# Rotating a matrix: half of one of the last outputs leaves through GpSimd in strips of seven partitions

## The chip, the core and the metric

One core of a Trainium2 chip runs the kernel. The metric is the time of one execution on the device, in microseconds (us), as the median of several runs; a profile of one execution shows where the time goes. The core has a matrix engine (TensorE, "PE" in the profile, with its weight loads as "PEld"), a vector engine (VectorE, "DVE"), ScalarE ("ACT"), GpSimd ("POOL") and SyncE ("SP"), and 16 DMA engines that move data between the DRAM and the on-chip memory (SBUF, 128 partitions). PSUM is the memory into which TensorE writes.

## The reference

```python
def setup_inputs():
    return {"x": np.random.randn(8192, 8192).astype(np.float32), "k": 1}

def reference(x, k):
    return np.rot90(x, k)
```

The 8192 x 8192 matrix of 4-byte numbers (268.4 MB) is turned by a quarter counterclockwise: `out[i, j] = x[j, 8191 - i]`. Nothing is computed. All of it is read once and written once, and within the chip each block is mirrored and transposed.

## The kernel before

**Tiles.** The input is cut into 16 macro blocks of R = 1024 rows by W = 4096 columns (`macros`, numbered kk). A macro block is loaded as T = 8 row strips of 128 rows, 2 MB each (`load`, L157), and leaves as J = 8 outputs of 2 MB. A strip consists of J = 8 pieces of CH = 512 columns; piece j of all 8 strips makes output j, so an output needs the whole macro block.

**Stages.** SyncE issues the loads into five buffers (`bufs`; LAND = 2 for loads, OUTS = 3 for outputs, with the roles mixed at the beginning and end by `load_buf` and `out_buf`). VectorE copies each strip piece by piece in reversed column order into `ring` (L209), which has 63 slots of 512 columns. TensorE transposes 128 x 128 blocks of the ring into PSUM (L241), 32 to an output, in two halves `ps0` and `ps1`. ScalarE copies each half to an output buffer (L272) and, when both are there, issues the store (L277). Semaphores order all of it: `s_land` for loads, `s_rev` for the reversed copies, `s_half` for a half transposed, `s_ev` for a half copied out, `s_store` for stores that have landed.

**The last macro block.** Its outputs are cut the other way so that work can begin with the first four strips: `outs` ends with t = 0 to 3 and columns j = (0, 1), (2, 3), (4, 5), (6, 7), and then t = 4 to 7 with the same columns. Each of these eight covers 1024 rows by 512 columns of the result, again 2 MB; partition m of the output buffer holds eight result rows m, m + 128 and so on, of 2 KB each. In an output with `js[0] == 0` the transposes are sorted by strip (L250), otherwise by block. The eight outputs use five buffers in turn (`ends` in `out_buf`), so the sixth, seventh and eighth wait at L268 for the store that used their buffer. These eight are "the last outputs" below, the fifth of them being the first one with t = 4 to 7.

**DMA.** `whole_reads` (L32) rewrites each load's and store's source so that a partition's 16 KB are read as one run. `LINE` and `HEAD` place the buffers in SBUF: `HEAD` is the width of the tile with the identity matrix, and the buffers' addresses are multiples of `LINE` bytes.

**GpSimd** writes the identity matrix (L174, L176) at the start and has nothing to do after that. SyncE ends with waits for every buffer's stores (L192).

Of the kernel before, what the change touches and what calls it, by code (L numbers as in the profile page):

```python
# [6 lines left out]
P = 128  # L7
# [5 lines left out]
G = 4  # L13
J = W // (G * P)
# [3 lines left out]
CH = G * P  # L18
F = G * R
SLOTS = T * J - 1  # L20

END = T // 2

H = 2
LAND = 2
OUTS = 3

LINE = 1024
HEAD = 224


def whole_reads(nc):  # L32

    for fn in nc.m.functions:
        for block in fn.blocks:
            for n, ins in enumerate(block.instructions):
                if not isinstance(ins, mybir.InstDMACopy):
                    continue
                src = ins.ins[0]
                ap = [list(d) for d in src.ap]  # L40
                if len(ap) == 3 and ap[2][0] == 1 and ap[1][0] == ap[2][1]:
# [12 lines left out]


def kernel(tc: tile.TileContext, x: bass.AP, k: bass.AP, out: bass.AP):
    nc = tc.nc
# [3 lines left out]
    N, M = x.shape  # L61
    dt = x.dtype
    macros = [(r0, c0) for r0 in range(0, N, R) for c0 in range(0, M, W)]
# [8 lines left out]
    for t in range(0, T, END):  # L72
        for j in range(0, J, wide):
            outs.append((KK - 1, range(t, t + END), range(j, j + wide)))
    assert len(outs) == n_out


    order = [(kk, a, b) for kk in range(KK) for a in range(T) for b in range(J)]
# [5 lines left out]
    with tc.tile_critical():  # L84
        head = nc.alloc_sbuf_tensor("head", [P, HEAD], dt)
        ident, scratch = head[:, :P], head[:, P : P + 1]
        bufs = [nc.alloc_sbuf_tensor(f"buf{i}", [P, F], dt) for i in range(LAND + OUTS)]
        ring = nc.alloc_sbuf_tensor("ring", [P, SLOTS * CH], dt)
        for b in bufs:
            assert nc.lookup_mloc(b).addr % LINE == 0  # L90
        ps = [
# [8 lines left out]
        s_first = nc.alloc_semaphore("s_first")  # L100
        s_half = nc.alloc_semaphore("s_half")
        s_ev = nc.alloc_semaphore("s_ev")

        def load_buf(m):
            if m < T:
# [1 line left out]
            return LAND + 2 if m == T else (m - T - 1) % LAND  # L107

        def out_buf(n):
            e = n - (n_out - J)  # L110
            if e < 0:
                return LAND + (n + 1) % OUTS
            ends = [load_buf(n_load - 2)]
            ends += [LAND + (n_out - J + i + 1) % OUTS for i in range(OUTS)]
            ends += [load_buf(n_load - 1)]
            return ends[e % len(ends)]

# [52 lines left out]
        with nc.Block() as block:  # L170

            @block.gpsimd
            def _(e):
                e.memset(ident, 0.0).then_inc(s_id, 1)  # L174
                e.wait_ge(s_id, 1)
                e.affine_select(  # L176
                    out=ident,
                    in_=ident,
                    compare_op=mybir.AluOpType.not_equal,
                    fill=1.0,  # L180
                    base=0,
                    pattern=[[-1, P]],
                    channel_multiplier=1,
                ).then_inc(s_id, 1)

            @block.sync
            def _(e):
                for m in range(LAND + OUTS, n_load):
                    last = [i for i in range(m) if load_buf(i) == load_buf(m)]
                    e.wait_ge(s_rev, rev[last[-1], J - 1])  # L190
                    load(e, m)
                for b in range(LAND + OUTS):  # L192
                    n = sum(out_buf(i) == b for i in range(n_out))
                    if n:
                        e.wait_ge(s_store[b], 16 * n)

            @block.vector
            def _(e):
                for m in range(n_load):
                    kk, t = divmod(m, T)  # L200
                    b = load_buf(m)
                    a = bufs[b][:].rearrange("p (j c) -> p j c", c=CH)
                    e.wait_ge(s_land[b], 16 * (uses_before(m, load_buf) + 1))
                    for lo, hi, wait in pieces[m]:
                        if wait:
# [12 lines left out]

            @block.tensor
            def _(e):  # L220
                seen = {}

                def wait(sem, n):
                    if seen.get(sem, 0) < n:
                        seen[sem] = n
                        e.wait_ge(sem, n)

                e.wait_ge(s_id, 2)
                for n, (kk, ts, js) in enumerate(outs):
                    blocks = [(j, g) for j in reversed(js) for g in range(G)]  # L230
                    half = len(blocks) // H
                    rows = len(ts) * P

                    def transpose(t, b):
                        j, g = blocks[b]
                        if n:
                            wait(s_ev, H * (n - 1) + b // half + 1)
                        wait(s_rev, rev[kk * T + t, j])
                        at = slot(kk, t, j) * CH + g * P
                        f = b % half * rows + (t - ts[0]) * P  # L240
                        i = e.transpose(  # L241
                            ps[b // half][:, f : f + P], ring[:, at : at + P], ident
                        )
                        if t == ts[-1] and b % half == half - 1:
                            i.then_inc(s_half, 1)
                        elif t == ts[0] and b == len(blocks) - 1:
                            i.then_inc(s_first, 1)

                    order = [(t, b) for b in range(len(blocks)) for t in ts]
                    if js[0] == 0:  # L250
                        order.sort()
                    for t, b in order:
                        transpose(t, b)

            @block.scalar
            def _(e):
                e.wait_ge(s_id, 2)
                e.copy(scratch, ident[:, :1])  # L258
                for n, (kk, ts, js) in enumerate(outs):
                    r0, c0 = macros[kk]  # L260
                    rows = len(ts) * P
                    b = out_buf(n)
                    for h in range(H):
                        if h == 0:
                            stores = uses_before(n, out_buf)
                            loads = [i for i in range(n_load) if load_buf(i) == b]
                            if stores:
                                e.wait_ge(s_store[b], 16 * stores)  # L268
# [3 lines left out]
                        e.copy(  # L272
                            bufs[b][:, h * F // H : (h + 1) * F // H], ps[h][:]
                        ).then_inc(s_ev, 1)
                    top = M - c0 - (js[-1] + 1) * CH
                    e.wait_ge(s_ev, H * (n + 1))
                    e.dma_start(  # L277
                        out=out[
                            top : top + len(js) * CH, r0 + ts[0] * P : r0 + ts[0] * P + rows
                        ].rearrange("(g m) f -> m g f", m=P),  # L280
                        in_=bufs[b][:].rearrange("m (g f) -> m g f", f=rows),
                    ).then_inc(s_store[b], 16)


# [33 lines left out]
```

## Time and profile before

| what | value |
|---|---|
| median of 3 runs | 1265.46 us (1265.02 to 1266.47) |
| the profiled execution's own time | 1265.5 us |
| its span in the profile | 1263.6 us |
| read from DRAM, written to it | 268.44 MB, 268.44 MB |
| loads (SyncE's queue) | 128 of 2 MB, landing 16.8 us after the issue at the median |
| stores (ScalarE's queue) | 128 of 2 MB, 25.7 us |
| reversed copies, 128 x 512 | 153, 418 ns each |
| PSUM copies, 128 x 2048 | 256, 1870 ns each |

The span is the time from the first to the last instruction of the program on the core; the time of an execution has some 2 us around it. A page of the profile gives busy times, 40 slices of the span, the transfers, and the chain of work that ended last; the trace behind it can be asked for single stretches of time. "Landing" is when a transfer's completion arrives.

### The profile page before, as it was taken

How to read it: one execution, taken by the hardware profiler on the slowest of the kernel's cores; microseconds unless marked ns; L12 is line 12 of the kernel's file. 1: busy time of each engine (PE TensorE's matmuls, PEld its weight loads, DVE VectorE, ACT ScalarE, POOL GpSimd, SP SyncE). 2: the span in 40 equal slices, each digit the busy share in tenths (PEclk: the TensorE clock that was granted, in tenths of full speed). 3: DMA queues.
4: the chain of work that ended last, by engine and by line, in shares of the span. 5: the costliest groups of instructions: out<-in, count | busy, mean ns of one | idle time of the engine just before them, and what ended most of it. 6: DMA issues, size and time to landing. Idle time of an engine off the chain costs nothing.

```text
span 1263.6 us, 9359 instructions
## 1 busy us (share of the span) xinstructions
PE 693.0 (55%) x4096; PEld 647.0 (51%) x4096; DVE 402.9 (32%) x313; ACT 467.0 (37%) x258; POOL 0.7 (0%) x6
## 2 busy tenths in 40 slices
PE   1556554665545655566555555555555555556563
PEld 1445454555545545565554554555445554455563
DVE  3323432234323343322342233422234222442210
ACT  0344333433344333433334333343333433434363
POOL 0000000000000000000000000000000000000000
PEclk9987767677677776767767777777776777767787
DMA  9999999999999999999999999999999999999998
GB/s 398 415 429 429 431 426 429 428 430 429 429 428 429 429 428 429 429 428 429 428 430 428 428 429 429 429 429 428 429 429 429 429 430 427 430 429 429 428 421 338
DMA packets 36904, 537.48 MB, mean 425 GB/s; under 512 B 4096, under 2 KB 4096, under 8 KB 4096
## 3 DMA queue, kind: packets, MB, share of 16 engines
q10 hardware_dynamic: 18432, 268.44, 50.0%
q1 hardware_dynamic: 18432, 268.44, 49.8%
q8 instruction: 32, 0.52, 0.2%
q14 instruction: 8, 0.07, 0.0%
HBM read 268.44 MB, written 268.44 MB: 425 GB/s over the span
## 4 chain that ended last, share of the span: by engine, by line
DMA 80%; issue 7%; ACT 5%; DVE 5%; PE 2%; ACTq 0%; SPq 0%
DMA buf<-in_x_dram 64%; DMA out_dram<-buf 16%; ACT buf L272 5%; DVE ring L209 5%; PE ps L241 2%; ACTq L277 0%; ACTq L271 0%; SPq L313 0%; SPq L84 0%
## 5 line engine op out<-in xcount | busy, mean ns | idle before, releaser
L241 PE MATMUL ps<-head,ring 128*128 128x128 f32 x4096 | 693.0, 346 | 550.7 <-ACT buf L272 472.8
L241 PEld LDWEIGHTS ps<-head,ring 128*128 128x128 f32 x4096 | 647.0, 184 | 596.5 <-ACT buf L272 511.5
L272 ACT COPY buf<-ps 128x2048 f32<-128x2048 f32 x256 | 465.5, 1870 | 778.2 <-DMA out_dram<-buf 594.8
L209 DVE COPY ring<-buf 128x512 f32<-128x512 f32 (+7 forms) x313 | 402.9, 1336 | 812.1 <-DMA buf<-in_x_dram 811.7
L258 ACT ACT_TABLE_LOAD x1 | 1.3, 1283 | 0.9 <-SPq L84 0.9
L176 POOL TENSOR_SCALAR_AFFINE_SELECT head<-head 128x128 f32<-128x128 f32 x1 | 0.3, 293 | 0.2 <-POOL head L174 0.2
L174 POOL MEMSET head<- 128x128 f32 x1 | 0.2, 204 | 0.5 <-SPq L84 0.5
L258 ACT COPY head<-head 128x1 f32<-128x1 f32 x1 | 0.2, 191 | 0.0
L299 POOL MEMSET const-bfloat16-1.0<- 128x1 bf16 x1 | 0.1, 101 | 0.0
L299 POOL MEMSET const-uint8-127<- 128x1 uint8 x1 | 0.1, 101 | 0.0
L299 POOL MEMSET const-float32-0.0<- 128x1 f32 x1 | 0.1, 98 | 0.2 <-issue 0.2
L299 POOL MEMSET const-float32-1.0<- 128x1 f32 x1 | 0.1, 98 | 0.0
## 6 DMA issues: line engine op xcount, KB each, us to landing
buf<-in_x_dram SPq DMA_DIRECT2D x128, 2048.0 KB, 16.8
out_dram<-buf ACTq DMA_DIRECT2D x128, 2048.0 KB, 25.7
```

The lines of the kernel that those rows point to most:

```text
L174: e.memset(ident, 0.0).then_inc(s_id, 1)
L176: e.affine_select(out=ident, in_=ident, compare_op=mybir.AluOpType.not_equal, fill=1.0, base=0, pattern=[[-1, P]], channel_multiplier=1,). ...
L209: i = e.tensor_copy(out=bass.AP(tensor=v.tensor, offset=v.offset, ap=[v.ap[0], [step * CH, n], [1, CH]],), in_=a[:, j : j + n, ::-1],)
L241: i = e.transpose(ps[b // half][:, f : f + P], ring[:, at : at + P], ident)
L258: e.copy(scratch, ident[:, :1])
L272: e.copy(bufs[b][:, h * F // H : (h + 1) * F // H], ps[h][:]).then_inc(s_ev, 1)
L299: nc = _bacc.Bacc("TRN2", target_bir_lowering=False, num_devices=1)
```

## The change

The eighth of the last outputs (j = 6, 7 with t = 4 to 7) is taken out of its place and put in the fifth, in two parts, so that there are now 129 entries in `outs`:

- Entry `n_few`: of the 512 columns j = 7, 448 are taken, as 16 groups of FEW = 28. VectorE writes them into the ring slot in groups 32 apart, reversed in order and within the group. TensorE transposes 64 columns at a time (two groups with their gaps), so that an output buffer has 64 partitions, of which 2 x 28 = 56 hold data, eight result rows of 2 KB each. ScalarE copies 64 partitions to the buffer and issues no store.
- Entry `n_few + 1`: the 512 columns j = 6 as before in four blocks, and the 64 left of j = 7, which VectorE writes into a new tile `extra`. ScalarE copies both and stores j = 6 alone (128 partitions x 4 rows, 1 MB).

GpSimd waits until all of this is in the buffers (`s_ev`), and then issues 24 transfers: eight times a filler (one number of the head tile copied within it), a store of seven partitions (every fourth of a group of 28, with eight 2 KB rows each, 112 KB), and a store of eight rows of 2 KB from the 64 left (16 KB). SyncE waits for these three kinds at the end. `whole_reads` leaves GpSimd's transfers alone. `LINE` becomes 256 and `HEAD` 160.

The remaining last outputs follow in their old order: j = (0, 1), (2, 3), (4, 5) with t = 4 to 7.

```diff
+FEW = 28
+SPLIT = 4
+EIGHTH = 32
-LINE = 1024
-HEAD = 224
+LINE = 256
+HEAD = 160
...
-                if not isinstance(ins, mybir.InstDMACopy):
+                if not isinstance(ins, mybir.InstDMACopy) or ins.engine == mybir.EngineType.Pool:
                     continue
...
     assert len(outs) == n_out
+    kk, ts, js = outs.pop()
+    n_few = n_out - END
+    ends = [js[-1], js[0]]
+    assert len(js) == 2 and END * P * H * G == F
+    few = [(ends[0], i * 2 * FEW, FEW) for i in range(H * G)]
+    rest = [(ends[0], H * G * 2 * FEW, CH - H * G * 2 * FEW)]
+    outs.insert(n_few, (kk, ts, js, [few[:G], few[G:]]))
+    outs.insert(n_few + 1, (kk, ts, js, [[(ends[1], g * P, P) for g in range(G)], rest]))
+    n_out += 1
+
+    def halves(n):
+        if len(outs[n]) == 4:
+            return outs[n][3]
+        blocks = [(j, g * P, P) for j in reversed(outs[n][2]) for g in range(G)]
+        return [blocks[: len(blocks) // H], blocks[len(blocks) // H :]]
...
+        extra = nc.alloc_sbuf_tensor("extra", [P, END * (CH - H * G * 2 * FEW)], dt)
...
         def out_buf(n):
-            e = n - (n_out - J)
+            e = n - (KK * J - J)
...
             @block.gpsimd
...
+                kk, ts, js, _ = outs[n_few]
+                b, c = out_buf(n_few), out_buf(n_few + 1)
+                top = M - macros[kk][1] - (js[-1] + 1) * CH
+                left = macros[kk][0] + ts[0] * P
+                rows = len(ts) * P
+                e.wait_ge(s_ev, H * (n_few + 2))
+                for i in range(2 * SPLIT):
+                    at, d = i // SPLIT * EIGHTH, i % SPLIT
+                    e.dma_start(
+                        out=head[:1, P + 8 + i : P + 9 + i], in_=head[:1, P : P + 1]
+                    ).then_inc(s_skip, 16)
+                    first = top + at // EIGHTH * FEW + d
+                    e.dma_start(
+                        out=bass.AP(
+                            tensor=out.tensor,
+                            offset=out[first : first + 1, left : left + 1].offset,
+                            ap=[[SPLIT * M, FEW // SPLIT], [2 * FEW * M, H * G], [1, rows]],
+                        ),
+                        in_=bufs[b][at + d : at + FEW : SPLIT].rearrange(
+                            "m (g f) -> m g f", f=rows
+                        ),
+                    ).then_inc(s_few, 16)
+                    first = top + rest[0][1] + i
+                    e.dma_start(
+                        out=out[first : top + CH : 8, left : left + rows],
+                        in_=bufs[c][i : 2 * EIGHTH : 8, G * rows : (G + 1) * rows],
+                    ).then_inc(s_rest, 16)
 
             @block.sync
...
+                e.wait_ge(s_few, 16 * 2 * SPLIT)
+                e.wait_ge(s_rest, 16 * 2 * SPLIT)
+                e.wait_ge(s_skip, 16 * 2 * SPLIT)
...
             @block.vector
...
+                        if kk == KK - 1 and t >= END and lo == J - 1:
+                            v = ring[:, slot(kk, t, lo) * CH :][:, :CH]
+                            i = e.tensor_copy(
+                                out=v.rearrange("p (g c) -> p g c", c=EIGHTH)[:, :, :FEW],
+                                in_=a[:, lo, CH - H * G * 2 * FEW :].rearrange(
+                                    "p (g c) -> p g c", c=FEW
+                                )[:, ::-1, ::-1],
+                            )
+                            width = CH - H * G * 2 * FEW
+                            i = e.tensor_copy(
+                                out=extra[:, (t - END) * width : (t - END + 1) * width],
+                                in_=a[:, lo, width - 1 :: -1],
+                            )
+                            i.then_inc(s_rev, 1)
+                            continue
...
             @block.tensor
...
+                        if n == n_few:
+                            width = 2 * EIGHTH
+                            at = slot(kk, t, j) * CH + b * width + h * G * width
+                            v = ring[:, at : at + width]
+                        elif n == n_few + 1 and h:
+                            at = (t - ts[0]) * width
+                            v = extra[:, at : at + width]
+                        i = e.transpose(ps[h][:width, f : f + P], v, ident)
...
             @block.scalar
...
+                        width = 2 * EIGHTH if n == n_few else parts[h][0][2]
+                        f = len(parts[h]) * rows
                         e.copy(
-                            bufs[b][:, h * F // H : (h + 1) * F // H], ps[h][:]
+                            bufs[b][:width, h * F // H : h * F // H + f], ps[h][:width, :f]
                         ).then_inc(s_ev, 1)
+                    if n == n_few:
+                        continue
...
+                    stores = [(top, 0, F // rows, P)]
+                    if n == n_few + 1:
+                        stores = [(top + CH, 0, G, P)]
```

More of the change, by code (lines that the diff above doesn't have):

```diff
@@ L102 @@
         s_ev = nc.alloc_semaphore("s_ev")
+        s_few = nc.alloc_semaphore("s_few")
+        s_rest = nc.alloc_semaphore("s_rest")
+        s_skip = nc.alloc_semaphore("s_skip")
         def load_buf(m):
@@ L113, in out_buf @@
             ends = [load_buf(n_load - 2)]
-            ends += [LAND + (n_out - J + i + 1) % OUTS for i in range(OUTS)]
+            ends += [LAND + (KK * J - J + i + 1) % OUTS for i in range(OUTS)]
             ends += [load_buf(n_load - 1)]
@@ L191, in _ @@
                     load(e, m)
+                e.wait_ge(s_few, 16 * 2 * SPLIT)
+                e.wait_ge(s_rest, 16 * 2 * SPLIT)
+                e.wait_ge(s_skip, 16 * 2 * SPLIT)
                 for b in range(LAND + OUTS):
-                    n = sum(out_buf(i) == b for i in range(n_out))
+                    n = sum(out_buf(i) == b and i != n_few for i in range(n_out))
                     if n:
@@ L228, in _, with transpose @@
                 e.wait_ge(s_id, 2)
-                for n, (kk, ts, js) in enumerate(outs):
-                    blocks = [(j, g) for j in reversed(js) for g in range(G)]
-                    half = len(blocks) // H
+                for n, (kk, ts, js, *_) in enumerate(outs):
+                    parts = halves(n)
                     rows = len(ts) * P
-                    def transpose(t, b):
-                        j, g = blocks[b]
+                    def transpose(t, h, b):
+                        j, off, width = parts[h][b]
@@ L236, in transpose @@
                         if n:
-                            wait(s_ev, H * (n - 1) + b // half + 1)
+                            wait(s_ev, H * (n - 1) + h + 1)
                         wait(s_rev, rev[kk * T + t, j])
[L239 to L244, printed above, removed]
+                        at = slot(kk, t, j) * CH + off
@@ new lines, in transpose @@
+                        f = b * rows + (t - ts[0]) * P
+                        v = ring[:, at : at + width]
+                        if n == n_few:
+                            width = 2 * EIGHTH
+                            at = slot(kk, t, j) * CH + b * width + h * G * width
+                            v = ring[:, at : at + width]
+                        elif n == n_few + 1 and h:
+                            at = (t - ts[0]) * width
+                            v = extra[:, at : at + width]
@@ L245, in transpose @@
+                        i = e.transpose(ps[h][:width, f : f + P], v, ident)
+                        if t == ts[-1] and b == len(parts[h]) - 1:
                             i.then_inc(s_half, 1)
-                        elif t == ts[0] and b == len(blocks) - 1:
+                        elif t == ts[0] and h == H - 1 and b == len(parts[h]) - 1:
                             i.then_inc(s_first, 1)
-                    order = [(t, b) for b in range(len(blocks)) for t in ts]
+                    order = [
+                        (t, h, b) for h in range(H) for b in range(len(parts[h])) for t in ts
+                    ]
@@ L250, in _ @@
                     if js[0] == 0:
                         order.sort()
-                    for t, b in order:
-                        transpose(t, b)
+                    for t, h, b in order:
+                        transpose(t, h, b)
             @block.scalar
@@ L258, in _ @@
                 e.copy(scratch, ident[:, :1])
-                for n, (kk, ts, js) in enumerate(outs):
+                for n, (kk, ts, js, *_) in enumerate(outs):
                     r0, c0 = macros[kk]
+                    parts = halves(n)
                     rows = len(ts) * P
@@ L264, in _ @@
                         if h == 0:
-                            stores = uses_before(n, out_buf)
+                            before = uses_before(n, out_buf)
                             loads = [i for i in range(n_load) if load_buf(i) == b]
-                            if stores:
-                                e.wait_ge(s_store[b], 16 * stores)
+                            if before:
+                                e.wait_ge(s_store[b], 16 * before)
                             elif loads:
@@ L271, in _ @@
                         e.wait_ge(s_half, H * n + h + 1)
+                        width = 2 * EIGHTH if n == n_few else parts[h][0][2]
+                        f = len(parts[h]) * rows
                         e.copy(
-                            bufs[b][:, h * F // H : (h + 1) * F // H], ps[h][:]
+                            bufs[b][:width, h * F // H : h * F // H + f], ps[h][:width, :f]
                         ).then_inc(s_ev, 1)
+                    if n == n_few:
+                        continue
                     top = M - c0 - (js[-1] + 1) * CH
+                    col = r0 + ts[0] * P
                     e.wait_ge(s_ev, H * (n + 1))
[L277 to L282, printed above, removed]
+                    stores = [(top, 0, F // rows, P)]
+                    if n == n_few + 1:
+                        stores = [(top + CH, 0, G, P)]
+                    for first, at, g, width in stores:
+                        e.dma_start(
+                            out=out[first : first + g * width, col : col + rows].rearrange(
+                                "(g m) f -> m g f", m=width
+                            ),
+                            in_=bufs[b][:width, at * rows : (at + g) * rows].rearrange(
+                                "m (g f) -> m g f", f=rows
+                            ),
+                        ).then_inc(s_store[b], 16)
 _INS = ['x', 'k']
```

## The prediction

> **What bounds the kernel now.** I read first the page's sums and slices, then the transfers, then the last 60 us.
>
> ```profile
> span 1263.6 us, 9359 instructions
> PE 693.0 (55%) x4096; PEld 647.0 (51%) x4096; DVE 402.9 (32%) x313; ACT 467.0 (37%) x258; POOL 0.7 (0%) x6
> ...
> DMA  9999999999999999999999999999999999999998
> ...
> DMA packets 36904, 537.48 MB, mean 425 GB/s; under 512 B 4096, under 2 KB 4096, under 8 KB 4096
> ```
>
> No compute engine is above 55%; the 16 DMA engines are full in every slice but the last. The end can therefore move only through the bytes (unchanged) or through how evenly the 16 engines run out. The packet count gives the unit of account: 256 transfers of 2 MB leave 16 small packets (their completions) and 128 large ones each, so 8 packets of 16 KB on each engine.
>
> The second view is busy time and DMA share in four stretches of the tail, each a whole number of packet times long (the last columns are DMA share and GB/s).
>
> ```profile
> 1250.00:1253.74 3.74, 0.00 (x0) 0.00 (x0) 0.00 (x0) 0.00 (x0) 0.00 (x0) 0.50 1.02 425
> 1254.70:1255.95 1.25, 0.00 (x0) 0.00 (x0) 0.00 (x0) 0.00 (x0) 0.00 (x0) 0.50 0.69 288
> 1256.60:1258.47 1.87, 0.00 (x0) 0.00 (x0) 0.00 (x0) 0.00 (x0) 0.00 (x0) 0.50 0.57 237
> 1260.34:1261.58 1.24, 0.00 (x0) 0.00 (x0) 0.00 (x0) 0.00 (x0) 0.00 (x0) 0.50 0.06 26
> ```
>
> 425 GB/s is 16 engines at 26.6 GB/s, so 16 KB take 0.62 us on one. Against 425, the other rows say 10.8, 8.9 and 1.0 engines: **five run dry by 1254.7, two more by 1256.6, eight by 1260.3, and one alone works until 1261.6**, where the packet records end. The whole stretch from 1250.00 has a share of 0.55 over 13.56 us, so the mean engine is done at 1250 + 7.46 = 1257.5. The kernel ends 4.1 us after a perfect division of the same work would. Nothing computes by then; what remains after 1261.6 is 1.96 us of landing and closing steps, which I keep.
>
> The third view is ScalarE's timeline, which shows when that work is handed over.
>
> ```profile
> 1222.81 3.63 ACT L272 COPY buf<-ps 128x2048 f32<-128x2048 f32 x2 [0.67 <-PE ps L241]
> 1226.48 0.99 ACTq L277 DMA_DIRECT2D out_dram<-buf  x1
> 1229.43 3.64 ACT L272 COPY buf<-ps 128x2048 f32<-128x2048 f32 x2 [2.98 <-PE ps L241]
> 1233.10 0.55 ACTq L277 DMA_DIRECT2D out_dram<-buf  x1
> 1233.74 3.63 ACT L272 COPY buf<-ps 128x2048 f32<-128x2048 f32 x2 [0.67 <-PE ps L241]
> 1237.40 0.55 ACTq L277 DMA_DIRECT2D out_dram<-buf  x1
> ...
> 1242.44 3.63 ACT L272 COPY buf<-ps 128x2048 f32<-128x2048 f32 x2 [0.76 <-PE ps L241]
> 1246.11 1.17 ACTq L277 DMA_DIRECT2D out_dram<-buf  x1
> ```
>
> The fourth to eighth of the last outputs are stored at 1226.5, 1233.1, 1237.4, 1241.7 and 1246.1. The 2.98 us before 1229.43 belong to the output that begins a group (columns j = 0, 1), whose transposes go row block by row block, so that its first half is complete only with its last.
>
> **The change, part by part.** *What each engine has to move.* The fifth stored output (j = 6, 7, t = 4 to 7) was one store: 8 packets per engine. Now half of it, j = 6, is stored as before: 4 packets' worth on each of 16. Of j = 7, 448 rows go in eight stores of seven partitions, 16 KB a partition; if a store is dealt out by whole partitions, as the 8 packets per engine show for 128, seven engines get eight 16 KB shares each. The other 64 rows go in eight stores of eight 2 KB rows: one share of 16 KB for each of eight engines. The fillers move 4 bytes. Against 8 packets, seven engines have 4 + 8 = 12 (+4, +2.5 us), eight have 5 (-3, -1.85 us), one has 4 (-4, -2.5 us). That is exactly the trace's count: seven early, eight late, one last. If each falls on its own group, the last ends at 1261.6 - 2.5 = 1259.1, the late ones by 1260.3 - 1.85 = 1258.5, and the early ones, by work alone, between 1257.2 and 1259.1.
>
> [...]
>
> *ScalarE and TensorE.* The split output leaves group order, so its first half is ready at 1224.73 + 16 x 0.117 (3.74 us for 32) = 1226.6, and ScalarE takes it after its issue, at 1227.5. Two copies of 64 x 2048: the row for 128 x 2048 is 1.82; I take it unchanged, the free size being the same (below by half at most). End 1231.1; no store of its own. The j = 6 half: 1231.2 to 1233.0; the 64 x 512 rest, a quarter of the length, 0.46 to 0.6: 1233.6. Its store is issued there. Then comes the group's first output, now sixth: + 2.98, + 3.64, issue 1240.25; the next two 4.3 us later each: 1244.6 and **1248.9, which is 2.8 us later than 1246.1**. Twenty more transposes (52 for the split output instead of 32) lie in these steps.
>
> *Whether the engines starve.* A last-group engine worked through 32 packets (19.9 us) after the fourth output, so an early engine is through with that at 1254.7 - 19.9 = 1234.8, a late one at about 1240. With 2.5 us of j = 6, early ones are empty at 1237.3, late ones at 1242.6. The sixth output's first packet comes at 1240.25 + 1.0 (the first load was issued at 0.95 and its first packet record stands at 1.96) = 1241.2. Late ones are covered; early ones have a hole of 3.9 us, in which only the first GpSimd shares can run.
>
> *GpSimd's 24 issues.* They wait for both halves of both outputs, 1233.6. No row prices a DMA issue on GpSimd. Its own rows are 0.10 to 0.29 us (memset, select), 24 x 0.29 = 7 us; ScalarE's issues have 0.55 at the median and 1.17 at most, 24 x 1.17 = 28 us. I take 0.99, the row at 1226.48, issued onto full engines as these are: 24 x 0.99 = 23.8, so the last is out at 1257.4 and its bytes pass by 1257.4 + 1.0 + 0.1 = 1258.5. A triple comes every 3.0 us; shares 0 and 1 reach the early engines at 1236.5 and 1239.5, in the hole, the other six later. Early engines then end at 1241.2 + 24 x 0.62 + 6 x 0.64 = **1259.9**. The 0.64 is 16 KB in eight rows of 2 KB; the trace's packet records have 0.626 for stores in 2 KB rows (0.611 for loads in one), and 0.6 to 0.8 bounds it, since reads are cut to 2 KB too. Completions and fillers are 32 packets of 9 ns by the same records: 0.3 us at most.
>
> [...]
>
> *VectorE.* Four 128x512 copies (0.42 us each) become a 448 and a 64 element copy, 0 to 0.42 us more each. The last ends at 1215.0, its output is first read at 1224.7: 9.7 us of cover; without that they would delay every later store by as much. Loads that wait for these copies come up to 0.42 us later while the DMA share stays at 1.00. The smaller head tile and 256-byte buffer alignment: nothing, between -0.1 and +0.5 us, packets of 16 KB remaining. The two buffers needed by the last outputs come free with the third and fourth output's landing, on the last engine 1261.6 - 19.9 = 1241.7 for the fourth and 5.0 earlier for the third; the copies that wait for them start at 1240.9 and 1245.2. Cover 3 us.
>
> *Sum.* Last packet at 1259.9 (early engines, the hole) against 1261.6: -1.7 us. The profiled execution took 1265.5 with its span of 1263.6, and the median of the runs is 1265.46, the same: **1263.8 us**, with 1263.0 if the last engine (1259.1) sets it.
>
> **The rivals.** *Dearer issues.* GpSimd's price p decides from 1.05 us on: the last packet stands at 1233.6 + 24p + 1.1. At 1.12 the gain is gone, at 1.225 the loss is 2.5 us, at 1.3 the last packet is at 1265.9 and the time 1269.8; at 1.5, 1274.6. For it: ScalarE's late issues took 0.99 and 1.17, and GpSimd has done nothing since 1.7 us. Against it: the 0.55 median.
>
> *Better than summed.* Issues of 0.6 us put five shares into the hole, and if the last engine's lag is also smaller, the end goes to the level of the mean. Floor: 1257.5, time 1261.4; likely 1262.6. Against it: the last engine is relieved of four packets and no more, 2.5 us, which alone is 0.2%.
>
> *Shares on the wrong engines.* Nothing in the trace names an engine; only the counts fit. If the seven fall on late engines, these end at 1260.3 + 2.5 = 1262.8 (1266.7); on the last one, 1264.1 (1268.0). [...]
>
> **How the numbers follow.** A run of this kernel can tell about 0.2%, 2.5 us, from no change. The forecast's case (1262.2 to 1265.2) has 0.47, of which 0.15 lies below 1262.9; better than summed 0.12; dearer issues 0.28; wrong engines 0.13, of which 0.04 stays within 2.5 us. Faster: 0.15 + 0.12 = 0.27. Same: 0.32 + 0.04 = 0.36. Slower: 0.28 + 0.09 = 0.37. The forecast's own range is 1262.2 to 1265.2; the one that holds 8 in 10 reaches from 1261.9 to 1269.5 (p of 1.29), leaving out the dearer half of the second case and the very floor.
>
> **What would show it.** Right: GpSimd's 24 issues within 24 us of 1233.6; the last store issued near 1248.9; a share of 1.0 up to some 1258 and a fall from 16 engines to none within 2 us, in place of the steps at 10.8, 8.9 and 1.0. A dip in the share at 1238 to 1241 would be the hole. Wrong: a last GpSimd store that lands alone, after ScalarE's; or a single engine that still works for 2.5 us by itself, which would mean that the filler missed it.

## The result, and the profile after

The changed kernel takes **1269.73 us** at the median of 7 runs (1268.90 to 1270.58), against 1265.40 (1265.02 to 1266.47, 7 runs) before: 4.3 us longer, a ratio of 1.0034 with a 95% interval of 1.0024 to 1.0044. The profiled execution took 1268.9 us with a span of 1267.0, 3.4 us more than before; it is the shortest of the seven, 0.8 under their median.

The page's sums and transfers after:

```profile
span 1267.0 us, 9431 instructions
PE 711.7 (56%) x4116; PEld 665.8 (53%) x4116; DVE 403.3 (32%) x317; ACT 469.5 (37%) x260; POOL 14.2 (1%) x30
...
DMA  9999999999999999999999999999999999999997
...
DMA packets 38056, 537.48 MB, mean 424 GB/s; under 512 B 4960, under 2 KB 4960, under 8 KB 5248
...
q0 software_dynamic: 1152, 1.05, 0.3%
```

The compute engines are as idle as before, and the bytes are the same. Queue q0 is GpSimd's: 1152 packets for 24 transfers, 72 for each of the 16 engines, although a filler moves 4 bytes and a store of seven partitions consists of seven shares of 16 KB.

Busy time and DMA share in stretches of the tail, before (the four stretches that the prediction showed are left out here) and after; the last two columns are DMA share and GB/s:

```profile
1234.00:1241.00 7.00, 5.86 (x51) 5.34 (x50) 0.00 (x0) 6.33 (x4) 0.00 (x0) 1.00 1.05 435
1241.00:1249.00 8.00, 2.70 (x25) 2.42 (x23) 0.00 (x0) 4.32 (x3) 0.00 (x0) 0.84 0.99 414
...
1250.00:1266.00 16.00, 0.00 (x0) 0.00 (x0) 0.00 (x0) 0.00 (x0) 0.00 (x0) 0.51 0.46 194
```

```profile
1234.00:1241.00 7.00, 5.43 (x50) 5.14 (x49) 0.00 (x0) 4.45 (x3) 7.00 (x13) 1.00 0.89 346
1241.00:1249.00 8.00, 4.29 (x37) 3.77 (x35) 0.00 (x0) 6.48 (x4) 5.74 (x11) 1.00 1.02 376
1250.00:1253.74 3.74, 0.00 (x0) 0.00 (x0) 0.00 (x0) 0.00 (x0) 0.00 (x0) 0.50 1.00 388
1254.70:1255.95 1.25, 0.00 (x0) 0.00 (x0) 0.00 (x0) 0.00 (x0) 0.00 (x0) 0.50 1.00 397
1256.60:1258.47 1.87, 0.00 (x0) 0.00 (x0) 0.00 (x0) 0.00 (x0) 0.00 (x0) 0.50 0.94 363
1260.34:1261.58 1.24, 0.00 (x0) 0.00 (x0) 0.00 (x0) 0.00 (x0) 0.00 (x0) 0.50 0.13 50
1250.00:1266.00 16.00, 0.00 (x0) 0.00 (x0) 0.00 (x0) 0.00 (x0) 0.00 (x0) 0.50 0.61 240
```

Two things are to be seen. First, the balance did come: where the share stood at 0.69 and 0.57 it is now 1.00 and 0.94. Second, the work as a whole runs later. After 1250 the engines are busy for 0.61 x 16 us = 9.8 us on average, against 0.46 x 16 = 7.4: **the mean engine is done 2.4 us later** (1259.8 instead of 1257.4) with the same bytes to move. The rows above say where that was lost: at 346 instead of 425 GB/s, 1234 to 1241 lost (1 - 346/425) x 7 = 1.3 us; at 376, 1241 to 1249 lost 0.9; at 388, 1250 to 1253.74 lost 0.3: 2.5 in all. In the first stretch the share fell too (0.89, engines with nothing to do); in the second it did not: at a share of 1.02 engines were occupied throughout and moved 12% less.

ScalarE's timeline and the first and last of GpSimd's issues, after:

```profile
1226.59 3.62 ACT L350 COPY buf<-ps 64x2048 f32<-64x2048 f32 x2 [0.83 <-PE ps L316]
1230.56 2.34 ACT L350 COPY buf<-ps 128x2048 f32<-128x2048 f32 x2 [0.35 <-PE ps L316]
1232.93 0.55 ACTq L362 DMA_DIRECT2D out_dram<-buf  x1
...
1239.56 0.55 ACTq L362 DMA_DIRECT2D out_dram<-buf  x1
...
1248.18 0.55 ACTq L362 DMA_DIRECT2D out_dram<-buf  x1
```

```profile
1233.20 0.67 POOL L216 DMA_DIRECT2D head<-head  x1 [1231.53 <-ACT buf L350]
1233.86 0.62 POOL L220 DMA_DIRECT2D out_dram<-buf  x1
1234.46 0.54 POOL L231 DMA_DIRECT2D out_dram<-buf  x1
...
1246.20 0.54 POOL L231 DMA_DIRECT2D out_dram<-buf  x1
```

Handing over went as foreseen or better: the last store of ScalarE at 1248.18, and all 24 issues of GpSimd out by 1246.7. What is late is not the issue but the landing. How long the stores of seven partitions (L220) took from issue to landing, after:

```profile
DMA to landing us min/median/max: 5.9/8.4/18.9
```

The last one issued takes the 18.9 us. The end, put together from the packet and semaphore records of the two traces:

| | before | after | grows by |
|---|---|---|---|
| last packet of ScalarE's stores ends | 1261.61 | 1262.25 | 0.64 |
| last packet of all ends (GpSimd's, after) | 1261.61 | 1262.72 | 0.47 |
| last landing | 1262.01 | 1264.66 | 1.54 |
| end of the span | 1263.56 | 1267.00 | 0.80 |

The four sum to the 3.45 us of the spans. GpSimd's last completions arrive 1.9 us after their last packet, where ScalarE's last one took 0.4; and after the last landing come 2.34 us instead of 1.55.

### The profile page after: what moved, and what is told of

The parts are those of the page before. It is cut to its first block, busy times and chain, and to the rows that moved or that the text cites. A ratio compares the mean times of both kernels' runs of the same rounds, so it can differ in the third digit from the quotient of the medians.

```text
span 1267.0 us, 9431 instructions
## 1 busy us (share of the span) xinstructions
PE 711.7 (56%) x4116; PEld 665.8 (53%) x4116; DVE 403.3 (32%) x317; ACT 469.5 (37%) x260; POOL 14.2 (1%) x30
## 3 DMA queue, kind: packets, MB, share of 16 engines
q10 hardware_dynamic: 18432, 267.40, 49.8%
q1 hardware_dynamic: 18432, 268.44, 49.6%
q0 software_dynamic: 1152, 1.05, 0.3%
## 4 chain that ended last, share of the span: by engine, by line
DMA 79%; issue 8%; DVE 5%; ACT 4%; PE 2%; ACTq 0%; SPq 0%
DMA buf<-in_x_dram 69%; DMA out_dram<-buf 10%; DVE ring L277 5%; ACT buf L350 4%; PE ps L316 2%; ACTq L362 0%; SPq L183 0%; ACTq L347 0%; SPq L400 0%; SPq L103 0%
## 5 line engine op out<-in xcount | busy, mean ns | idle before, releaser
L316 PE MATMUL ps<-head,ring 128*128 128x128 f32 x4112 | 711.3, 352 | 534.1 <-ACT buf L350 464.1
L316 PEld LDWEIGHTS ps<-head,ring 128*128 128x128 f32 x4112 | 665.4, 187 | 579.8 <-ACT buf L350 502.6
L216 POOL DMA_DIRECT2D head<-head x8 | 4.5, 560 | 1231.5 <-ACT buf L350 1231.5
L220 POOL DMA_DIRECT2D out_dram<-buf x8 | 4.9, 612 | 0.0
L231 POOL DMA_DIRECT2D out_dram<-buf x8 | 4.3, 542 | 0.0
## 6 DMA issues: line engine op xcount, KB each, us to landing
out_dram<-buf ACTq DMA_DIRECT2D x1, 1024.0 KB, 12.3
```

Of the source, the lines that this page charges most:

```text
L216: e.dma_start(out=head[:1, P + 8 + i : P + 9 + i], in_=head[:1, P : P + 1]).then_inc(s_skip, 16)
L220: e.dma_start(out=bass.AP(tensor=out.tensor, offset=out[first : first + 1, left : left + 1].offset, ap=[[SPLIT * M, FEW // SPLIT], [2 * FE ...
L231: e.dma_start(out=out[first : top + CH : 8, left : left + rows], in_=bufs[c][i : 2 * EIGHTH : 8, G * rows : (G + 1) * rows],).then_inc(s_r ...
L316: i = e.transpose(ps[h][:width, f : f + P], v, ident)
```

## The experiments

Four theories stood at first. **T**: GpSimd's packets take turns with ScalarE's 16 KB packets on each engine, so that its backlog, and with it the end, is set by their number. **C**: once GpSimd has issued any transfer, the program closes more slowly. **H**: the new order leaves engines idle while the group that begins with j = 0, 1 is held back. **M**: which engines get GpSimd's shares decides. Later came **P**: stores of fewer partitions than 128 slow the 16 KB packets; and against it **N**: more transfers cost time by themselves. Differences below are of medians, against runs of the kernel before on the same chip (1265.33 to 1265.42).

### Fillers alone: one at the start, 24 early, 24 late

Before, with transfers of one number that GpSimd issues, and SyncE's wait for them at the end; nothing else changes. One at the start:

```diff
+                e.wait_ge(s_id, 2)
+                e.dma_start(
+                    out=head[:1, P + 8 : P + 9], in_=head[:1, 0:1]
+                ).then_inc(s_skip, 16)
```

and 24 when the fifth of the last outputs is in its buffer; for the early ones the wait is `H * (n_out - 2 * J)`; they were issued 137 to 124 us before the end, and their last packet ended 80 us before it:

```diff
+                e.wait_ge(s_ev, H * (n_out - END + 1))
+                for i in range(24):
+                    e.dma_start(
+                        out=head[:1, P + 8 + i : P + 9 + i], in_=head[:1, P : P + 1]
+                    ).then_inc(s_skip, 16)
```

> The kernel before with one 4-byte GpSimd transfer at the start, waited for at the end. Theory C (a program with any GpSimd transfer closes more slowly: in the trace after, 2.3 us lie between the last landing and the end of the span, 1.55 before): 1266.2 us. Theory T (GpSimd's packets take turns with ScalarE's 16 KB packets and land last) and theory H (the new order of the last outputs leaves DMA engines idle around 1237 to 1243): no difference, 1265.4 us.

> The kernel before with 24 GpSimd transfers of 4 bytes when the fifth of the last outputs is in its buffer; nothing of the order or of the division of the stores is changed. Theory T: each transfer leaves two packets on every engine, 48 turns, and some 43 packets of 16 KB are still to come, so they end with ScalarE's last and land late: 1267 to 1268 us. Theory H: 1265.4 us. Theory C: 1266.2 us.

> The kernel before with 24 GpSimd transfers of 4 bytes, issued when 112 of the 128 outputs are in their buffers, so that they are over long before the end. Theory T in its form 'they land last and the closing waits for them': no loss, 1265.4 us. In its form 'each packet slows the 16 KB packets beside it' (the trace of the run with late fillers has 8 us of longer packets over 16 engines): 1265.9 us.

One: 1265.16 us (ratio 0.9998, 0.9990 to 1.0007). 24 late: 1267.10 (1.0014, 1.0005 to 1.0023), +1.7. 24 early: 1265.90 (1.0005, 0.9996 to 1.0014), not told apart from nothing. It is the very number that had been given for packets that slow those beside them, but the records don't show that: from 1126 to 1190, 2 of 1667 packets of 16 KB took over 0.75 us, and 2 of 1674 before. C falls: with the one and with the 24 early ones the program closes in 1.54 and 1.55 us after the last landing, as before. The late ones, from the page of that run:

```profile
q0 software_dynamic: 768, 0.00, 0.0%
...
L188 POOL DMA_DIRECT2D head<-head x24 | 12.4, 524 | 1234.1 <-ACT buf L279 1234.1
...
head<-head POOLq DMA_DIRECT2D x24, 0.0 KB, 8.5
```

A transfer of 4 bytes leaves 32 packets (768 for 24), two for each engine, and lands 8.5 us after its issue at the median. The last landed at 1263.37, 0.95 after ScalarE's last, and the span ended 2.35 us later still. So the packets cost nothing by their bytes; most of the loss is that they land late. (That profiled execution also had a stretch of a lower TensorE clock, 0.76 in 1227 to 1234; its own time, 1267.85, is the longest of its 11.)

### After without its fillers

```diff
-                    e.dma_start(
-                        out=head[:1, P + 8 + i : P + 9 + i], in_=head[:1, P : P + 1]
-                    ).then_inc(s_skip, 16)
```

> The changed kernel without its eight fillers: 16 GpSimd transfers. The packets per engine fall from 72 to 56, and if transfers are dealt to successive engines, each pair now begins one engine earlier (7 + 8 = 15 of 16), so the seven and eight shares spread over all engines instead of falling on a chosen group. Theory T: fewer turns, 1269.2 us. Theory M (the placement by the filler brings a relief that is merely covered up): 1270.5 us or more. If neither counts: 1269.7 us.

1266.74 us (1.0014, 1.0006 to 1.0023): **3.0 us faster than after**, far more than the 0.5 that T had given it. From its page, and the landing of its stores of seven partitions:

```profile
q0 software_dynamic: 896, 1.05, 0.3%
```

```profile
DMA to landing us min/median/max: 5.9/6.2/14.2
```

Now GpSimd queues 56 packets per engine instead of 72, and its last landing is at 1257.06, before ScalarE's at 1262.98; the span ends 1.67 us after that, close to the 1.55 of before. With the 16 turns, the additions of the table that belong to GpSimd (0.47, 1.54, 0.80) are gone but for 0.12 us in the closing. What remains is +1.4 us against before; ScalarE's own last packet ends at 1262.58, 0.33 later than in after. The fillers' issues are gone too, so that GpSimd's last issue was out at 1242.7 instead of 1246.7; but its packets went on for 13.9 and 16.0 us after that, so that it was the queue that ended late and not the issuing.

### An option on the transfers, and one place later

The first sets an option on all of GpSimd's transfers (`single_packet=True`); the second puts the split output sixth (`n_few = n_out - END + 1`), after the group's first output.

> The changed kernel with each GpSimd transfer's share of an engine in one packet (8 rows of 2 KB in one packet of 16 KB instead of four of 4 KB; padding likewise). Theory T: packets per engine and triple fall from 9 to 6, so the last lands earlier: 1267.5 to 1268.7 us. Theories H and C: as the changed kernel, 1269.7 us.

> The changed kernel with the split output in sixth place instead of fifth, so that ScalarE's store of the group's first output goes out at 1233 us as in the kernel before, and no idle stretch should open in the DMA share. Theory H (the idle stretch at 1237 to 1243 is a part of the loss, 1.8 us by the run with SyncE's stores): 1267.9 us, give or take 0.5. Theory T alone (turns of GpSimd's packets and their late landing make the loss): GpSimd begins 6.6 us later, so 1269.7 us or more.

1269.54 us (1.0034, 1.0021 to 1.0046) and 1270.09 (1.0036, 1.0024 to 1.0049). The option left the packet count at 1152, so that run says nothing on T. The second is 0.4 above after where H had 1.8 below it; the last GpSimd landing is at 1265.90, later with the later start, as T has it.

### The order alone, and the split stored without GpSimd

The first takes before and moves its last output to the fifth place, whole. The second is after with GpSimd's stores replaced by three from SyncE, of 28, 28 and 64 partitions.

```diff
     assert len(outs) == n_out
+    outs.insert(n_out - END, outs.pop())
```

> Before with the eighth of the last outputs (j = 6, 7 with t = 4 to 7) put in the fifth place, whole, stored by ScalarE in one transfer of 128 partitions; nothing is split and GpSimd stores nothing. H (the order leaves an idle stretch, as the group that begins with j = 0, 1 is held back): the stores that follow come 1 to 2 us later than in before and cost 0.5 to 1.9 us, 1266 to 1267.3. Against it, the cost of the run in which SyncE stored the split part (1267.2) lies in the split, in stores of 28 and 64 partitions that collide, and the order alone is worth nothing: 1265.0 to 1265.8.

> The changed kernel with its order and its split, but the 448 and 64 rows are stored by SyncE in three transfers (twice 28 partitions, once 64) instead of GpSimd's 24. No relief of single engines is meant here. Theory H: the idle stretch stays, 1267.5 us or more. Theory T: most of the loss is gone, 1265.4 to 1266.5 us.

The order alone: 1265.30 us (1.0001, 0.9992 to 1.0009), nothing. H falls. The split without GpSimd: 1267.24 (1.0016, 1.0007 to 1.0025), +1.85, between what T and H had given it. So a loss of the size that stayed without fillers comes with the split, whoever stores it. In that trace 23 of SyncE's 56 packets of 16 KB took 0.75 us or more, up to 2.04, against 0.626 for the usual one.

### Where the shares fall

Three ways to move GpSimd's shares to other engines. The first two are after without fillers, the 64 left rows as one transfer of one row and seven of nine (`piece(lo, n)` stores n rows seven apart from row lo); in the second the one row comes last and each piece of nine stands ahead of its seven. The first:

```diff
+                piece(0, 1)
                 for i in range(2 * SPLIT):
...
-                    e.dma_start(
-                        out=out[first : top + CH : 8, left : left + rows],
-                        in_=bufs[c][i : 2 * EIGHTH : 8, G * rows : (G + 1) * rows],
-                    ).then_inc(s_rest, 16)
+                    if i < 7:
+                        piece(1 + i, 9)
```

The third is after, with eight more fillers that GpSimd issues at its start:

```diff
+                for i in range(8):
+                    e.dma_start(
+                        out=head[:1, P + 16 + i : P + 17 + i], in_=head[:1, :1]
+                    ).then_inc(s_skip, 16)
```

> After without its fillers, and the 64 left rows are stored in one transfer of one row and seven of nine rows (partitions seven apart) instead of eight of eight: one row first, then seven partitions, nine rows, seven partitions, and so on, 16 GpSimd transfers as in the run without fillers. The number of packets per engine on GpSimd's queue is that run's, 56, so T (packets of GpSimd take turns with the 16 KB packets and land last) expects that run's 1266.7 us, between 1266.0 and 1267.7, if where the shares fall is worth nothing. M (a placement that comes round to the same seven engines relieves the late ones) expects the time below that run by 1 us or more, 1264.0 to 1265.7, since 1 + 7 + 9 + 7 + 9 brings each store of seven partitions to the same seven engines with no filler.

> The same 16 transfers in another order: nine rows first, then seven partitions, and so on, the one row at the end, so that, if the engines are taken in turn, all stores of seven partitions fall on seven engines that the run before did not use for them. T: no difference to the run with the one row first, both near 1266.7 us. M: the two differ by 1.5 us or more, with this one the slower (1267 to 1269) if the run before hit the early engines, or the faster if the seven there were late ones.

> After with eight more transfers of one number each, issued by GpSimd at its very start. They are done a thousand microseconds before the tail, where 24 of them 100 us or more before the end cost nothing that could be measured. If the engines are taken in turn, they move every later share by eight engines: the stores of seven partitions then fall on seven of the engines that had the pieces of eight rows. M (the time depends on which engines get the shares, and after's choice is the one that fits): the seven fall on engines that run late, which end 2 to 4 us after the rest: 1271.5 to 1274. If after's choice is the one that does not fit, the time falls to 1266 to 1268. T (the end is set by the number of GpSimd's turns behind 16 KB packets and by their late landing, the same on every engine): 1269.0 to 1270.4, as after.

1267.51 us (1.0017, 1.0008 to 1.0026), 1267.56 (1.0019, 1.0010 to 1.0028) and 1270.05 (1.0040, 1.0026 to 1.0053). The first two agree to 0.05 us, both 0.8 above after without fillers, and the third is after's again. No run gave M anything. But M isn't refuted as a mechanism. The trace doesn't name engines; where one record begins as exactly one other ends, though, the two can be put on one engine, and so it can be seen for a part of the shares of rows (2 KB packets) what GpSimd's store before them left on that engine. After a store of seven partitions, 9 of 15 shares of nine rows in the first run follow a 4096-byte packet: these engines carry shares of both kinds, so the stores did not come round as intended. In the third run, as in after, the engine that ends last is one with the eight-row pieces, so that nothing shows that the shares moved. In after all of 20 eight-row shares follow an 8-byte packet, and in after without fillers all of 18. So the two kinds stood on separate engines with the fillers and without them: the fillers were not needed for that, and the 3.0 us between these two runs do not come from mixing them.

### How a store is cut

All on ScalarE's queue, with no GpSimd transfer: on before, the very last store in 120 and 8 partitions; on the order-only kernel, the moved output's store in two by columns, 128 partitions each, and in two by partitions, 64 each.

```diff
+                    m_cuts = [0, P]
+                    if n == n_out - 1:
+                        m_cuts = [0, P - 8, P]
```

```diff
+                    if n == n_out - END:
+                        cuts = [(slice(0, P), slice(0, G)), (slice(0, P), slice(G, 2 * G))]
```

```diff
+                    if n == n_out - END:
+                        cuts = [(slice(0, P // 2), slice(None)), (slice(P // 2, P), slice(None))]
```

> The kernel before with its very last store cut into one of 120 partitions and one of 8, both from ScalarE; GpSimd and the order as before. If a store is dealt by whole partitions over the largest number of engines up to 16 that divides them, 120 go to 15 engines at 8 packets each, and one engine is spared 8 packets, 5 us. If the engine that works alone until 1261.6 us is the spared one, the end is set by the next at 1260.4 to 1261: 1264.2 to 1264.9 us. If it is another, 1265.4 us, and 1266.0 where the 8 partitions fall on it.

> The order-only run (the eighth of the last outputs whole in the fifth place), with that output's store cut into two transfers of 128 partitions by 8 KB. Theory P (packets of partitions that are dealt to the engines otherwise slow each other): every engine still reads the partitions that it reads in all other stores, so nothing is lost, 1265.0 to 1265.8, and no 16 KB packet takes over 0.75 us. Theory N (a store cut in more transfers costs time by itself): 1266 or more.

> The same with the store cut into two transfers of 64 partitions by 16 KB, with four packets for each engine in each. P: an engine now reads other partitions than in the stores around it, while another engine reads the same range, so 16 KB packets above 0.75 us appear while these transfers run, and the time is 1265.7 to 1267.5. N: as the run cut by columns, whatever that is. If neither costs anything, the loss of the split runs needs the uneven counts of partitions, 28 and 120.

120 and 8: 1267.10 us (1.0016, 1.0007 to 1.0025), +1.8: one engine is spared (a share of 15 in 16 in 1250 to 1254), but 30 of 192 packets of 16 KB after 1250 took over 0.75 us, and the time is above everything that had been given for it. (SyncE's stores of 28, 28 and 64 partitions fit a dealing like that of the 120: they left 44 packets under 512 bytes, 4140 in all against 4096 before, as one for each of 14, 14 and 16 engines would.) By columns: 1265.43 (0.9999, 0.9990 to 1.0008), nothing. **By partitions: 1271.27 us (1.0044, 1.0032 to 1.0057), +5.85**, more than the whole change. N falls; P has the sign of both, though the second lies 3.8 us above its range. Windows of the run by columns:

```profile
1234.00:1241.00 7.00, 4.61 (x29) 4.38 (x28) 0.00 (x0) 4.33 (x3) 0.00 (x0) 0.76 1.01 421
1241.00:1249.00 8.00, 4.70 (x41) 4.18 (x39) 0.00 (x0) 6.58 (x4) 0.00 (x0) 1.00 0.99 414
...
1250.00:1266.00 16.00, 0.00 (x0) 0.00 (x0) 0.00 (x0) 0.00 (x0) 0.00 (x0) 0.51 0.48 199
```

and of the run by partitions:

```profile
1234.00:1241.00 7.00, 4.93 (x31) 4.69 (x30) 0.00 (x0) 5.38 (x3) 0.00 (x0) 0.77 1.00 360
1241.00:1249.00 8.00, 4.67 (x40) 4.19 (x38) 0.00 (x0) 5.04 (x4) 0.00 (x0) 0.93 0.98 322
...
1250.00:1266.00 16.00, 0.00 (x0) 0.00 (x0) 0.00 (x0) 0.00 (x0) 0.00 (x0) 0.50 0.64 268
```

The share is full in both (1.01 and 0.99 by columns, 1.00 and 0.98 by partitions), but one moves 421 and 414 GB/s and the other 360 and 322: **busy is not moving**. The mean engine's end follows: 0.64 x 16 = 10.2 us after 1250 against 7.7. The packet records put a count to it; all packets of 16 KB from 1230 on:

| run | loss, us | packets above 0.75 us | time above 0.626, us of one engine |
|---|---|---|---|
| before | 0 | 1 of 699 | 0.5 |
| order alone | -0.1 | 1 of 701 | 0.5 |
| two by columns | 0.0 | 0 of 571 | 0.4 |
| 24 fillers late | +1.7 | 17 of 710 | 7.9 |
| after without fillers | +1.4 | 37 of 560 | 12.3 |
| 120 and 8 | +1.8 | 31 of 705 | 18.4 |
| split stored by SyncE | +1.85 | 32 of 636 | 19.6 |
| two by partitions | +5.85 | 73 of 706 | 43.8 |
| after | +4.3 | 47 of 563 | 17.9 |

Every run in which a tail store covers only part of the partitions has the slow packets. (The five such runs that are not in the table have 23 to 52 of 571 to 578.) Of those without one only the late fillers bring a number of them, so that in after the two causes are mixed: without its fillers 12.3 of its 17.9 us are left. One engine's time is a sixteenth of the kernel's: 17.9 us are 1.1 us for each, and the 43.8 of the run by partitions are 2.7. The profiled execution of that run took 1269.13, the shortest of its five (the longest 1272.93), 3.7 us over before; what the other 2.1 of the 5.85 are, its trace can't show. No version was found that beats the kernel before.

## Why the prediction was wrong

It gave 1263.8 us, 1.7 less than before, and ended its range at 1269.5; the kernel takes 1269.7.

**What held.** The mean engine's end before, 1257.5, is 1257.4 by the long stretch. ScalarE's last store came at 1248.18 for a forecast 1248.9, GpSimd's start at 1233.2 for 1233.6. 16 KB in eight rows take 4 x 0.16 = 0.64 us, as estimated. The shares came in the numbers foreseen: 224 packets of 4096 bytes, four for each of seven shares in eight stores, and 64 of 2 KB, eight for each of eight pieces. That the engines are taken in turn, so that each kind falls on one group every time and on the group meant, was assumed and is not shown, as the trace names no engine; the records that can be put on one engine have the two kinds on separate ones in after (20 of 20) and partly on the same in the first run with pieces of nine rows (9 of 15). The dip in the share at 1234 to 1241 was forecast as a hole, and it is there; but the run with the order alone has a share of 1.00 in the same stretch, so its cause is the split and not, as the prediction had it, the later sixth store alone.

**Issue price.** 24 issues took 13.5 us, 0.56 each, against the 0.99 taken. "Dearer issues", the rival for slower, is refuted: it had the sign and not the cause. The issues were out 11 us before the prediction's 1257.4, and the end did not move forward with them, because they were not what came last. The 1.0 us from issue to first packet was too little for GpSimd: its first packet began at 1236.59, 3.4 us after its first issue (4.0 for the one filler at the start).

**The step that failed: "Completions and fillers are 32 packets of 9 ns by the same records: 0.3 us at most."** The count was wrong and the price was of the wrong kind. GpSimd's queue moved 1152 packets: 576 of 4 bytes, 288 of 8, 64 of 2 KB and 224 of 4096 bytes. Divided by 16 engines that is 72 each, and the counts fit two from a filler, two from an eight-row piece and five from a seven-partition store, of which four are 4096 bytes on seven engines (28 to a store) and 8 bytes on the nine others (36). And a packet's price is not its 9 ns but its turn: while both queues have work, the records that can be put on one engine alternate one for one between a 16 KB packet and one of GpSimd's, of whatever size; starts of the 16 KB packets are 0.622 us apart alone, 0.627 with a 4-byte packet between, 0.78 with one of 4096 bytes. (Of the 59 packets of 2 KB or 4096 bytes that GpSimd's queue began between 1250 and 1260 in after, 42 begin where a 16 KB packet ends and end where another begins, and 13 more do one of the two, to within 5 ns.) So the small ones cost ScalarE next to nothing, and GpSimd's queue up to 0.63 us each. Sixteen turns fewer (after without fillers) brought GpSimd's last packet from 1262.72 to 1256.63, 6.1 us forward.

**The 1.96 us that the prediction kept** for landing and closing became 4.28 (1262.72 to 1267.00), and this is the larger half of the loss: 1.54 in the late completion, 0.80 in the closing. The landing records show what the completion's part is made of. On the engine that ends last, GpSimd's queue still held the completions of 11 transfers when ScalarE's last packet was done. Their packets were over within 0.47 us, but they landed one every 0.19 us after ScalarE's last landing at 1262.57: 1262.57 + 11 x 0.19 = 1264.66. With 24 late fillers 5 were left (1262.42 + 5 x 0.19 = 1263.37), with the split one place later 14 (from 1263.25 to 1265.90), without fillers none. The 11 x 0.19 = 2.09 us are nearly all of the two additions 0.47 and 1.54, and each transfer that is still behind the last large packet costs 0.19 us in these runs. The closing grows where GpSimd's transfers land last (2.34 after, 2.35 with 24 late fillers) and not where ScalarE's do (1.55 before and with one filler or 24 early ones, 1.67 without fillers and 1.66 with the split stored by SyncE). In the instruction records the growth lies between SyncE's last drain and GpSimd's own last event, 0.85 us apart after and 0.03 before; why, the trace doesn't show. That the last GpSimd store would land alone, after ScalarE's, stood in the prediction as a sign of being wrong; it was given no price, and that is what came.

**The relief of the last engine** was forecast as 1261.6 to 1259.1, bounded by the early engines at 1259.9. ScalarE's last packet ended at 1262.25. The division did improve: from mean to last there were 4.2 us before and 2.45 after, 1.75 less, close to the 1.7 forecast. It was measured against a mean that had moved 2.4 us, which the prediction held fixed by pricing every 16 KB packet at 0.62 whatever else was stored beside it. Shown is that a store cut by partitions does this and one cut by columns does not. Why is not shown. In the run by partitions the extra transfer left 16 more packets on ScalarE's queue (18448 instead of 18432), as one completion for each of 16 engines would, so half of the partitions seem to go over all 16 engines too. That an engine then reads partitions which other engines read at the same time, and that this slows both, was the author's guess in theory P; it fits the runs, but no record says which engine reads which partition. Another cause is as open: a cut by partitions also changes which rows of the result are written at the same time, and no run separates the two ends of the transfer.

**In sum**, about 3.0 of the 4.3 us go with the fillers (after against after without fillers), through their turns and what lands behind them, and 1.4 with the split, which is the slow packets and the dip less the gain in balance. What stays open: which engine ends last and whether other shares would help it; why the closing grows by 0.8 us; how a cut by partitions slows the packets; and the 0.8 us by which the median lies above the profiled execution.

## What to carry to other kernels

Count a small transfer by its packets on every engine and by its turns behind the large packets, not by its bytes (here 32 packets for 4 bytes, and up to 0.63 us a turn); if it must be late, have as few of them as can be and see that they do not land last. Where a store must be cut while others run, try its columns first: here each cut across partitions cost 1.4 to 5.85 us, and the one along columns nothing. Read the DMA share together with GB/s: a share of 0.98 at 322 GB/s is a loss that the share alone hides. Before buying balance with extra transfers, price what they do to the mean.

## What the runs showed of the hardware

- 24 GpSimd transfers of 4 bytes left 768 packets, 32 each or two for each of 16 engines. The 24 transfers of after left 1152, of them 576 of 4 bytes and 288 of 8; a store of seven partitions has 28 packets of 4096 bytes, and the 8-byte ones come to 36 for each.
- GpSimd issues such transfers back to back at 0.52 to 0.67 us each (after and 24 late fillers); in after the first packet began 3.4 us after the first issue.
- While ScalarE's and GpSimd's queues both had work, the packet records that can be put on one engine alternated one for one: starts of the 16 KB packets were 0.622 us apart alone, 0.627 with a 4-byte packet between and 0.78 with one of 4096 bytes, and 42 of 59 packets of 2 KB or 4096 bytes stood between two of 16 KB.
- At the end of the program ScalarE's last completion came 0.3 to 0.4 us after its last packet; the GpSimd completions behind it landed 0.19 us apart, 5, 11 or 14 of them; and the closing took 2.34 and 2.35 us where GpSimd's landed last, against 1.54 to 1.67 where ScalarE's did.
- Two stores of 64 partitions in place of one of 128 cost 5.85 us, and 73 of 706 packets of 16 KB from 1230 on took over 0.75 us, up to 2.58, where 0.626 is usual. Two of 128 partitions and half the columns cost nothing (1265.43 us against 1265.42 before).
